# Writing the bulk loads of a row-maximum kernel with 32 KB source pieces over 16 KB destination rows

## The chip, the cores and the metric

One core of one Trainium2 chip. The time is microseconds of device time for one execution of the program; the span of the profile is about 1.8 us shorter, because it begins and ends with the instructions. All runs told here are of granted clock 1.0 on the one core.

## The reference

```python
def setup_inputs():
    batch, seq, dim = 32, 512, 1024
    return {"x": np.random.randn(batch, seq, dim).astype(np.float32)}

def reference(x):
    return np.max(x, axis=-1).astype(np.float32)
```

So 16384 rows of 4 KB (67.1 MB) are read once, and one number comes out of each row.

## The kernel before

Four consecutive rows (16 KB, contiguous in memory) go to each of the 128 partitions, which makes a tile of 2 MB. There are 32 tiles: 28 bulk ones, loaded and reduced whole, and four at the end, loaded in halves of 1 MB. Up to eight bulk loads are in flight.

```python
G = 4
xr = xf.rearrange("(t p g) d -> t p g d", p=P, g=G)
bulk = ctx.enter_context(tc.tile_pool(name="bulk", bufs=10))
...
for t in range(T):                       # T = 32
    if t < T - 4:
        xc = bulk.tile([P, G, D], F32)
        nc.sync.dma_start(out=xc, in_=xr[t])
        nc.vector.reduce_max(out=res[:, :, t], in_=xc, axis=X)
    else:
        for h in range(0, G, 2):
            xt = tailp.tile([P, 2, D], F32)
            nc.sync.dma_start(out=xt, in_=xr[t, :, h:h + 2, :])
            nc.vector.reduce_max(out=res[:, h:h + 2, t], in_=xt, axis=X)
# cut: four small transposes of the maxima and four stores
```

Of the kernel before, what the change touches and what calls it, by code (L numbers as in the profile page):

```python
# [1 line left out]

# [4 lines left out]


F32 = mybir.dt.float32
G = 4  # L10


@with_exitstack
def kernel(
    ctx: ExitStack,
    tc: tile.TileContext,
    x: bass.AP,
    out: bass.AP,
):
    nc = tc.nc  # L20
    P = 128
    X = mybir.AxisListType.X

    xf = x.flatten_outer_dims()
    N, D = xf.shape
    T = N // (P * G)


    xr = xf.rearrange("(t p g) d -> t p g d", p=P, g=G)
    of = out.flatten_outer_dims()  # L30

    bulk = ctx.enter_context(tc.tile_pool(name="bulk", bufs=10))
    tailp = ctx.enter_context(tc.tile_pool(name="tailp", bufs=5))
    once = ctx.enter_context(tc.tile_pool(name="once", bufs=1))


    res = once.tile([P, G, T], F32)
    turned = once.tile([P, 32, G], F32)

    for t in range(T):  # L40
        if t < T - 4:
            xc = bulk.tile([P, G, D], F32)
            nc.sync.dma_start(out=xc, in_=xr[t])  # L43
            nc.vector.reduce_max(out=res[:, :, t], in_=xc, axis=X)  # L44
        else:
            for h in range(0, G, 2):
# [4 lines that stand above are left out]
    for g in range(G):  # L51
        nc.vector.transpose(out=turned[:, :, g], in_=res[:, g, :])  # L52

    for q in range(P // 32):
        dst = bass.AP(
            tensor=of.tensor,
            offset=of.offset + q * 32 * G,
            ap=[[P * G, T], [1, 32 * G]],
        )
        eng = (nc.scalar, nc.sync)[q % 2]  # L60
        eng.dma_start(out=dst, in_=turned[q * 32:(q + 1) * 32, :, :].rearrange("p a g -> p (a g)"))


# [1 line left out]
_INS = ['x']  # L65
_OUTS = [((32, 512), 'float32')]


# [23 lines left out]
```

## Time and profile before

| | before |
|---|---|
| time, median of 4 runs | 168.15 us (167.98 to 168.31) |
| span of the profile | 166.3 us |
| VectorE busy | 142.0 us |
| a bulk reduction | 4.421 us |
| from one bulk reduction to the next | 4.894 us |
| last bulk reduction starts | 140.72 us |

The period of 4.894 us is worked out from the trace: the first bulk reduction starts at 8.580 us, the 28th at 140.719, and (140.719 - 8.580) / 27 = 4.894. All periods below are taken in this way.

From the page of the kernel before: the busy tenths of the DMA engines in 40 slices, the bytes moved, the packets, the queues, and the largest group of VectorE (busy us, mean ns | idle us just before, and who ended it):

```profile
DMA  5999999999999999999999999999999999999930
GB/s 177 402 433 437 441 437 429 410 426 441 433 429 414 426 441 433 426 414 429 441 433 422 422 426 441 433 422 422 426 441 433 422 418 418 422 424 420 422 154 16
DMA packets 5376, 67.18 MB, mean 404 GB/s; under 512 B 640, under 2 KB 768, under 8 KB 768
...
q1 hardware_dynamic: 5280, 67.14, 95.5%
...
L44 DVE TENSOR_REDUCE res<-xc 128x4 f32<-128x4096 f32 x28 | 123.8, 4421 | 21.3 <-DMA xc<-in_x_dram 21.3
```

The DMA engines are busy 90% or more of every slice between the first and the last two, and VectorE waits for them before every bulk reduction. The chain of waits that ended last (start us, us, what) says the same:

```profile
2.12 21.09 DMA xc<-in_x_dram
...
23.27 39.10 DMA xc<-in_x_dram
...
62.44 39.08 DMA xc<-in_x_dram
...
101.58 39.11 DMA xc<-in_x_dram
...
140.72 4.42 DVE res L44
145.14 15.36 DVE res L49 x7
```

One piece of the chain is one load from its issue to its landing, with eight loads in flight: eight tiles land in each 39.1 us. After the last bulk tile VectorE works without a pause to the end. Time taken off the period of a bulk load should therefore come off the total, 28 times, as long as VectorE still has to wait for it.

### The profile page before, as it was taken

Reading aid. Unit: us, or ns where it says so; the run is one execution under the profiler, and the core shown is the slowest. Engines: PE = TensorE matmul, PEld = TensorE weight load, DVE = VectorE, ACT = ScalarE, POOL = GpSimd, SP = SyncE. Lnnn points to the kernel's source line nnn. Section 1 sums busy time; section 2 is a strip of 40 time slices with the busy share of each in tenths; the row PEclk is TensorE's granted clock in tenths of the full one; section 3 lists DMA queues with packets and bytes.
Section 4 is the critical chain, followed back from the end, with each engine's and each line's share of the span. In section 5 each row is a group of like instructions: output and inputs, shape, how many; then the busy total and the mean of one; then the engine's idle time right before and its main releaser. Section 6 shows DMA issues by size and latency. Waiting matters only on the chain.

```text
span 166.3 us, 147 instructions
## 1 busy us (share of the span) xinstructions
DVE 142.0 (85%) x40; POOL 0.2 (0%) x4
## 2 busy tenths in 40 slices
DVE  0098888898888889888889988888988888999992
POOL 0000000000000000000000000000000000000000
DMA  5999999999999999999999999999999999999930
GB/s 177 402 433 437 441 437 429 410 426 441 433 429 414 426 441 433 426 414 429 441 433 422 422 426 441 433 422 422 426 441 433 422 418 418 422 424 420 422 154 16
DMA packets 5376, 67.18 MB, mean 404 GB/s; under 512 B 640, under 2 KB 768, under 8 KB 768
## 3 DMA queue, kind: packets, MB, share of 16 engines
q1 hardware_dynamic: 5280, 67.14, 95.5%
q10 hardware_dynamic: 96, 0.03, 0.1%
HBM read 67.11 MB, written 0.07 MB: 404 GB/s over the span
## 4 chain that ended last, share of the span: by engine, by line
DMA 83%; DVE 14%; SPq 1%; issue 0%; DVEq 0%
DMA xc<-in_x_dram 83%; DVE res L49 11%; DVE res L44 3%; SPq L43 1%; DVE turned L52 0%; DVEq L87 0%
## 5 line engine op out<-in xcount | busy, mean ns | idle before, releaser
L44 DVE TENSOR_REDUCE res<-xc 128x4 f32<-128x4096 f32 x28 | 123.8, 4421 | 21.3 <-DMA xc<-in_x_dram 21.3
L49 DVE TENSOR_REDUCE res<-xt 128x2 f32<-128x2048 f32 x8 | 17.7, 2274 | 0.0
L52 DVE STREAM_TRANSPOSE turned<-res 128x32 f32<-128x32 f32 x4 | 0.7, 213 | 0.1
L76 POOL MEMSET const-bfloat16-1.0<- 128x1 bf16 x1 | 0.1, 101 | 0.0
L76 POOL MEMSET const-uint8-127<- 128x1 uint8 x1 | 0.1, 101 | 0.0
L76 POOL MEMSET const-float32-0.0<- 128x1 f32 x1 | 0.1, 98 | 0.2 <-issue 0.2
L76 POOL MEMSET const-float32-1.0<- 128x1 f32 x1 | 0.1, 98 | 0.0
## 6 DMA issues: line engine op xcount, KB each, us to landing
xc<-in_x_dram SPq DMA_DIRECT2D x28, 2048.0 KB, 39.1
xt<-in_x_dram SPq DMA_DIRECT2D x8, 1024.0 KB, 28.3
out_dram<-turned SPq DMA_DIRECT2D x2, 16.0 KB, 1.5
out_dram<-turned ACTq DMA_DIRECT2D x2, 16.0 KB, 1.6
```

Of the source, the lines that this page charges most:

```text
L43: nc.sync.dma_start(out=xc, in_=xr[t])
L44: nc.vector.reduce_max(out=res[:, :, t], in_=xc, axis=X)
L49: nc.vector.reduce_max(out=res[:, h:h + 2, t], in_=xt, axis=X)
L52: nc.vector.transpose(out=turned[:, :, g], in_=res[:, g, :])
L76: nc = _bacc.Bacc("TRN2", target_bir_lowering=False, num_devices=1)
```

## The change

Let each bulk load read memory in 64 pieces of 32 KB, each of which covers the rows of two neighbouring partitions, while every partition still receives 16 KB. The DMA engines would then handle half as many source pieces (the prediction calls them read descriptors).

```diff
-    xr = xf.rearrange("(t p g) d -> t p g d", p=P, g=G)
-    of = out.flatten_outer_dims()
+    def stretch(first, rows):
+        piece = 8192
+        return bass.AP(
+            tensor=xf.tensor,
+            offset=xf.offset + first * D,
+            ap=[[piece, rows * P * D // piece], [1, piece]],
+        )
 ...
         if t < T - 4:
             xc = bulk.tile([P, G, D], F32)
-            nc.sync.dma_start(out=xc, in_=xr[t])
+            nc.sync.dma_start(out=xc.rearrange("p g d -> p (g d)"), in_=stretch(t * P * G, G))
             nc.vector.reduce_max(out=res[:, :, t], in_=xc, axis=X)
```

(`xr` stays, for the tail, and so does `of`; both only move. Blank lines are left out.)

More of the change, by code (lines that the diff above doesn't have):

```diff
@@ L38 @@
     turned = once.tile([P, 32, G], F32)
+    xr = xf.rearrange("(t p g) d -> t p g d", p=P, g=G)
     for t in range(T):
```

## The prediction

> **What bounds the kernel.** The loads. The chain of waits that ended last is 83% "DMA xc<-in_x_dram" and 14% VectorE; VectorE is busy 142.0 of 166.3 us, and each of its 28 bulk reductions takes 4421 ns after some 0.48 us of waiting for a load (21.3 us in all, 8.6 of it before the first). The chain walks in steps of 39.10 us for 8 tiles: one 2 MB tile lands every 4.888 us, 429 GB/s. Only after the last bulk tile lands (140.7 us) is VectorE the limit: 4.4 us for that tile, eight tail reductions back to back (2.27 us each), transposes and the store.
>
> **What the change touches.** Only the read side of the 28 bulk loads: 64 source pieces of 32 KB instead of 128 of 16 KB. Bytes, destinations, issue order, waits, buffers and VectorE work stay (the order of instructions is identical). The Trainium skill, "DMA: Bandwidth & Descriptors", section "Why a DMA increments its semaphore by 16 and not by 1", says the engine count is the largest up to 16 that divides both sides' slowest dimension: 64 and 128 still give 16. I expect each engine to keep the same bytes and the same eight partitions, with 4 reads per tile instead of 8.
>
> **What there is to gain.** The trace's DMA records: a 16 KB packet takes 611 to 619 ns, an 8 KB packet 309 to 313, a 4-byte completion write 9. Extrapolating (estimate: 2 x 309 - 611) gives some 7 ns fixed per descriptor. A second estimate: the same page's "Where 436 GB/s comes from" puts the ceiling at 435.2 GB/s, or 4.819 us per tile; the trace shows 4.888, so 69 ns per tile are overhead: 8 x 7.5 ns plus the 9 ns completion.
>
> If the fixed cost belongs to the read descriptor, halving the reads saves 4 x 7.5 = 30 ns per tile, 28 x 30 = 0.84 us. If it belongs to the write descriptor, or the hardware cuts the pair at the smaller piece, nothing is saved. The floor (no overhead at all) would be 28 x 69 ns = 1.9 us, so over 2% faster (3.4 us) is nearly excluded.
>
> **On the critical path.** All of any saving: the last bulk tile lands earlier by the sum, and the VectorE tail, which follows without idle time, starts that much earlier. VectorE (4.42 us) stays under the load period (4.86). The start (first reduction at 8.6 us) should be unchanged or a tenth or two worse, because the first reads (0.8 to 1.8 us in the trace) become larger.
>
> **Prediction.** 167.5 us (range 166.6 to 168.5), from 168.14. Faster by over 2%: 0.02; within 2%: 0.94; slower by over 2%: 0.04.
>
> **What would show it.** 1792 bulk records of 32 KB near 1215 ns (or still 3584 of 16 KB if records count writes); landings every 4.86 us instead of 4.888 (38.9 for 8 tiles); VectorE idle before bulk reductions down to about 20.5 us; last bulk reduction starting near 139.9 instead of 140.7; the tail of 22.3 us unchanged.
>
> **What would make it wrong.** [...] If a 32 KB read against two 16 KB writes stalls the engine, packets would exceed 2 x 614 ns and the kernel be a per cent or so slower. If the period is unchanged, the fixed cost sits on the write side.

## The result, and the profile after

168.19 us (168.14 to 168.27, 4 runs) against 168.15 us: ratio 1.0003, 95% interval 0.9985 to 1.002. Here and below, a ratio is the mean time of one kernel's runs over the mean of the other's from the same rounds, so it is not quite the ratio of the medians quoted beside it.

The same lines of the page of the kernel after, with the same columns:

```profile
DMA  5999999999999999999999999999999999999930
...
DMA packets 5376, 67.18 MB, mean 404 GB/s; under 512 B 640, under 2 KB 768, under 8 KB 768
...
q1 hardware_dynamic: 5280, 67.14, 95.5%
...
L53 DVE TENSOR_REDUCE res<-xc 128x4 f32<-128x4096 f32 x28 | 123.8, 4422 | 21.4 <-DMA xc<-in_x_dram 21.4
```

And its chain of waits:

```profile
23.35 39.11 DMA xc<-in_x_dram
...
62.52 39.10 DMA xc<-in_x_dram
...
101.68 39.10 DMA xc<-in_x_dram
...
140.81 4.42 DVE res L53
145.23 15.36 DVE res L58 x7
```

Nothing moved: the same number of packets to the last one, the same steps of 39.1 us, the same idle time. A count that does not change by a single packet, after an edit that was to halve 3584 reads, asks for a look at what was built. The records of the transfers show 3584 packets of 16 KB in both traces. The built program explains it. The access patterns of the first bulk load, written as [step, count] in elements, slowest first, are:

```
before   source [[4096, 128], [1, 4096]]   destination [[4096, 128], [1, 4096]]
after    source [[4096, 128], [1, 4096]]   destination [[4096, 128], [1, 4096]]
```

All 28 bulk loads are like this. A comparison of the two built programs, instruction by instruction, found no difference except the places in the source (line numbers and call stacks). The load call brings both sides of a transfer to one form before it makes the instruction; the 64 stretches of 32 KB lie end to end in memory, so they were cut again to match the 128 destination rows. **The edit never reached the chip, so this run says nothing about 32 KB reads.** The ratio of 1.0003 is that of a program to itself, and so a measure of the noise.

That leaves the question that the edit was meant to ask. I had three theories for it. R: the fixed cost of a piece belongs to the read side, so that real 32 KB reads would save time. W: it belongs to the write side. N: no fixed cost per piece sets the period.

### The profile page after: what moved, and what is told of

Read it like the earlier page. It is cut to its first block, busy times and chain, and to the rows that moved or that the text cites. A ratio compares the mean times of both kernels' runs of the same rounds, so it can differ in the third digit from the quotient of the medians.

```text
span 166.4 us, 147 instructions
## 1 busy us (share of the span) xinstructions
DVE 142.0 (85%) x40; POOL 0.2 (0%) x4
## 2 busy tenths in 40 slices
DMA packets 5376, 67.18 MB, mean 404 GB/s; under 512 B 640, under 2 KB 768, under 8 KB 768
## 3 DMA queue, kind: packets, MB, share of 16 engines
q1 hardware_dynamic: 5280, 67.14, 95.5%
## 4 chain that ended last, share of the span: by engine, by line
DMA 83%; DVE 14%; SPq 1%; issue 0%; DVEq 0%
DMA xc<-in_x_dram 83%; DVE res L58 11%; DVE res L53 3%; SPq L52 1%; DVE turned L61 0%; DVEq L96 0%
## 6 DMA issues: line engine op xcount, KB each, us to landing
xc<-in_x_dram SPq DMA_DIRECT2D x28, 2048.0 KB, 39.1
```

## The experiments

The pattern can be put into the instruction after the front end has made it. The following block stands in the launch code, just before the program is handed over, and gives the 28 bulk loads a source and a destination pattern of choice. It also turns off the flag `ant_dge_precooked`, because the front end had set it for its own pattern. Below, each experiment gives only SRC and DST.

```diff
+    import copy
+    for block in (bl for f in nc.m.functions for bl in f.blocks):
+        for k, ins in enumerate(block.instructions):
+            if type(ins).__name__ == "InstDMACopy" and [list(d) for d in ins.ins[0].ap] == [[4096, 128], [1, 4096]]:
+                block.instructions[k] = copy.replace(
+                    ins,
+                    ins=[copy.replace(ins.ins[0], ap=SRC)],
+                    outs=[copy.replace(ins.outs[0], ap=DST)],
+                    ant_dge_precooked=False,
+                )
     r = _run(nc, [arrays], core_ids=[0])
```

What could not be tried: reads smaller than the writes. Reads of 8 KB or 1 KB against 16 KB rows do not compile ("DMA instruction must read and write same number of elements (or, for a plain HW-DGE copy, read elements that are whole multiples of the write element)"). Reads of 64 KB failed at the same place. So the read side can only be made equal to the write side or wider.

### Real 32 KB reads, and their control

read32_write16 (from the kernel after):

```diff
-SRC = [[4096, 128], [1, 4096]]
+SRC = [[8192, 64], [1, 8192]]
 DST = [[4096, 128], [1, 4096]]
```

> In the built program the changed kernel is identical to the one before: the front end turned the 64 pieces of 32 KB back into 128 reads of 16 KB. This run writes the pattern [64 pieces x 8192 elements] into the 28 bulk instructions after the build, so that the reads really are 32 KB (flag ant_dge_precooked off). Theory R (fixed cost on the read side): 8 to 4 reads per engine and tile, landings every 4.858 us instead of 4.888, about 0.84 us less than read16_write16_plain (0.995). Theory W (fixed cost per write, or per piece both sides are cut to) and theory N (no fixed cost sets the period): equal within 0.1%, landings every 4.888 us. If the engines' share of the destinations does not follow the wider reads, the result is wrong[...].

read16_write16_plain (from the kernel before; only the flag is changed):

```diff
 SRC = [[4096, 128], [1, 4096]]
 DST = [[4096, 128], [1, 4096]]
-ant_dge_precooked=True
+ant_dge_precooked=False
```

> Control: the kernel before with the same rewriting of the 28 bulk instructions but unchanged patterns, only the flag ant_dge_precooked off. All theories: 168.15 us within 0.3 us, landings every 4.888 us; the issue of one bulk load on the queue of SP may take longer than 0.33 us, which eight loads in flight hide except at the start.

Measured on one chip, both results right: 168.42 us with 32 KB reads, 168.47 us for the control, 168.12 us for the kernel before. Against before the ratios are 1.0015 (1.0002 to 1.0027) and 1.0016 (1.0003 to 1.0029). From the page of read32_write16:

```profile
DMA packets 3585, 67.18 MB, mean 403 GB/s; under 512 B 641, under 2 KB 769, under 8 KB 769
...
q1 hardware_dynamic: 3488, 67.14, 95.1%
...
L53 DVE TENSOR_REDUCE res<-xc 128x4 f32<-128x4096 f32 x28 | 123.8, 4422 | 21.6 <-DMA xc<-in_x_dram 21.6
```

and two steps of its chain of waits:

```profile
23.59 39.09 DMA xc<-in_x_dram
...
62.75 39.09 DMA xc<-in_x_dram
```

Now the reads are 32 KB: queue q1 has 3488 packets instead of 5280, exactly 1792 fewer, and the transfer records show 1792 of 32 KB with a median of 1.227 us in the steady part, twice the 0.611 to 0.619 us of a 16 KB record. So the packets of a trace count reads. The steps are still 39.09 us, and the period is 4.894 us (control 4.896). The same lines of the control read16_write16_plain:

```profile
L44 DVE TENSOR_REDUCE res<-xc 128x4 f32<-128x4096 f32 x28 | 123.8, 4422 | 21.7 <-DMA xc<-in_x_dram 21.7
```

```profile
23.62 39.10 DMA xc<-in_x_dram
...
62.79 39.10 DMA xc<-in_x_dram
```

Theory R asked for 30 ns less per tile and 0.84 us in all; 2 ns and 0.05 us were found, and 0.05 us is less than the spread of either kernel's five runs. R falls.

The right result and the unchanged period also agree with the prediction's reading of the Trainium skill, "DMA: Bandwidth & Descriptors", section "Why a DMA increments its semaphore by 16 and not by 1": 64 source pieces and 128 partitions still spread over all 16 engines (the packets of q1 fill 95.1% of the time of 16 engines, against 95.5% in the kernel before).

The control explains the 0.3 us by which both lose: issuing one bulk load takes 472 ns on the queue of SP instead of 328, and the long wait of the chain starts at 2.60 us instead of 2.12. That is the flag, not the reads.

### Smaller writes, with and without smaller reads

read16_write1 (from the kernel before):

```diff
-SRC = [[4096, 128], [1, 4096]]
-DST = [[4096, 128], [1, 4096]]
+SRC = [[4096, 128], [1, 1], [1, 4096]]
+DST = [[4096, 128], [256, 16], [1, 256]]
```

> Reads stay 16 KB, each is written in 16 pieces of 1 KB (same destination bytes). Theory W: 120 more write pieces per engine and tile at about 7.5 ns, an estimate from the first trace: +0.9 us per tile, landings every 5.8 us, about 193 us in all. Theory R: landings every 4.888 us, 168.2 us. Theory N: the same 168.2 us.

read1_write1 (from the kernel before):

```diff
-SRC = [[4096, 128], [1, 4096]]
-DST = [[4096, 128], [1, 4096]]
+SRC = [[4096, 128], [256, 16], [1, 256]]
+DST = [[4096, 128], [256, 16], [1, 256]]
```

> Both sides in 1 KB pieces. Theory W (cost per write only, or per pair of pieces): the same as read16_write1, about 193 us. Theory R (reads alone cost): about 193 us while read16_write1 stays at 168.2. If both sides cost on their own: slower than read16_write1. Theory N: 168.2 us.

Measured: 199.83 us (ratio 1.1885) and 199.97 us (ratio 1.1894), both right. The pages, first read16_write1:

```profile
DMA packets 5376, 67.18 MB, mean 339 GB/s; under 512 B 640, under 2 KB 768, under 8 KB 768
...
L44 DVE TENSOR_REDUCE res<-xc 128x4 f32<-128x4096 f32 x28 | 123.8, 4422 | 53.0 <-DMA xc<-in_x_dram 53.0
```

then read1_write1:

```profile
DMA packets 59136, 67.18 MB, mean 339 GB/s; under 512 B 640, under 2 KB 58112, under 8 KB 58112
...
L44 DVE TENSOR_REDUCE res<-xc 128x4 f32<-128x4096 f32 x28 | 123.8, 4422 | 53.4 <-DMA xc<-in_x_dram 53.4
```

Three landings from the timeline of read16_write1 (start us, us; the interval is the period):

```profile
64.01 4.42 DVE L44 TENSOR_REDUCE res<-xc 128x4 f32<-128x4096 f32 x1 [1.59 <-DMA xc<-in_x_dram]
70.04 4.42 DVE L44 TENSOR_REDUCE res<-xc 128x4 f32<-128x4096 f32 x1 [1.61 <-DMA xc<-in_x_dram]
76.06 4.42 DVE L44 TENSOR_REDUCE res<-xc 128x4 f32<-128x4096 f32 x1 [1.59 <-DMA xc<-in_x_dram]
```

The second kernel has 11 times as many packets as the first and is no slower beyond 0.14 us in 200. The first has not one packet more than the kernel before and is 32 us slower. The number that the page prints is the number of reads, and here it is not the one that matters. The periods are 6.022 and 6.023 us against 4.896 of the control. With 128 writes per engine and tile instead of 8, that is (6.022 - 4.896) us / 120 = 9.4 ns per write. Theories R and N fall; W stays, with 9.4 ns in place of the 7.5 that I had estimated (the reason why both runs came out at 200 and not at 193 us).

One thing this does not show: that a short read is free. In every kernel here the reads are as long as the writes or longer. A cost of reads that runs beside the writes and is no larger than theirs would stay hidden, and no run excludes it.

### Is it a fixed time per write?

read16_write4 (from the kernel before):

```diff
-SRC = [[4096, 128], [1, 4096]]
-DST = [[4096, 128], [1, 4096]]
+SRC = [[4096, 128], [1, 1], [1, 4096]]
+DST = [[4096, 128], [1024, 4], [1, 1024]]
```

> Is the cost of a write piece one fixed time? From the two 1 KB runs: (6.022 - 4.896) us / 120 extra write pieces per engine and tile = 9.4 ns each. Reads of 16 KB written in 4 pieces of 4 KB are 24 extra pieces: +0.225 us, bulk reductions every 5.121 us, 28 x 0.225 = 6.3 us more than read16_write16_plain, about 174.8 us. If small pieces cost more each than large ones, less: at 2 ns a piece 169.8 us.

Measured: 174.61 us (ratio 1.039), right. The period is 5.120 us, so (5.120 - 4.896) us / 24 = 9.3 ns per extra write of 4 KB: the same price as for 1 KB. (This run was made on another chip than its control; the kernel before took 168.07 us on this chip and 168.12 us on the control's.) A cost of the longer pattern as such, whatever the number of writes, is excluded by the two results: 1.126 us for 120 extra writes and 0.224 us for 24 lie on a straight line through zero, within 2 ns. From its page:

```profile
L44 DVE TENSOR_REDUCE res<-xc 128x4 f32<-128x4096 f32 x28 | 123.8, 4421 | 27.8 <-DMA xc<-in_x_dram 27.8
```

The transfer records of the engines say the same: the median record of a 16 KB read takes 614 ns with one write (control), 644 ns with four and 756 ns with sixteen, which is 10 and 9.5 ns per extra write.

This run also answers an objection to W, that the queue which makes the descriptors is the slow part. The start of its chain of waits:

```profile
0.73 0.63 SPq L43
...
1.42 0.58 SPq L43
...
2.05 0.59 SPq L43
...
2.68 0.66 SPq L43
...
3.39 1.80 SPq L43
...
5.24 4.87 SPq L43
```

The first four loads, together 4 x 512 = 2048 writes, were issued in 2.6 us; only then was the queue held up. The fifth issue took 1.80 us, and the next ones nearly a whole period each. So 2048 writes, as many as one load of the 1 KB kernels has, are issued in less than half of the 6.02 us which such a load takes. As far as the times of issue tell, the queue waits for the engines, not the engines for the queue. A slow queue working beside the transfers would also show only when it became slower than they are, while this cost is there from 24 extra writes on.

### Larger writes

With four rows per partition no write can be longer than 16 KB. A load of 4 MB with eight rows per partition allows 32 KB. Both kernels below read 32 KB and differ only in the writes. They put the maxima of the two halves where those of two tiles belonged. Their outputs are wrong, which doesn't matter for the times.

Both (from the kernel before):

```diff
+    xw = xf.rearrange("(t p g) d -> t p g d", p=P, g=2 * G)
-    bulk = ctx.enter_context(tc.tile_pool(name="bulk", bufs=10))
+    bulk = ctx.enter_context(tc.tile_pool(name="bulk", bufs=5))
 ...
         if t < T - 4:
-            xc = bulk.tile([P, G, D], F32)
-            nc.sync.dma_start(out=xc, in_=xr[t])
-            nc.vector.reduce_max(out=res[:, :, t], in_=xc, axis=X)
+            if t % 2:
+                continue
+            xc = bulk.tile([P, 2 * G, D], F32)
+            nc.sync.dma_start(out=xc, in_=xw[t // 2])
+            nc.vector.reduce_max(out=res[:, :, t], in_=xc[:, :G, :], axis=X)
+            nc.vector.reduce_max(out=res[:, :, t + 1], in_=xc[:, G:, :], axis=X)
```

tile4m_write16 has besides (the block above, for the 14 loads of 4 MB):

```diff
+SRC = [[8192, 128], [1, 1], [1, 8192]]
+DST = [[8192, 128], [4096, 2], [1, 4096]]
```

> Control of tile4m_write32; the rows of each pair of tiles land in another order, so the result is wrong on purpose. One load of 4 MB for two tiles, cut into 16 KB writes (reads of 32 KB): a pair of tiles should land every 2 x 4.896 = 9.78 to 9.79 us. Total about 172.5 us: the last bulk load leaves two reductions of 4.42 us to do instead of one.

tile4m_write32 has instead:

```diff
+SRC = [[8192, 128], [1, 8192]]
+DST = [[8192, 128], [1, 8192]]
```

> The same with writes of 32 KB, which one partition row of the 4 MB tile holds; result wrong on purpose as in its control. If the fixed cost is 9.4 ns per write piece and still holds there: 8 pieces fewer per engine and load, 75 ns less of 9.78 us, over 14 loads 1.05 us less than tile4m_write16 (ratio 0.994). If the cost were not a fixed time per piece but only of small pieces: equal within 0.1%. Under the read theory, which the earlier runs speak against: equal, as both read 32 KB.

Measured: 172.35 us and 171.21 us (ratios to the kernel before 1.0253 and 1.0186). A step of the chain of waits is four loads of 4 MB here; tile4m_write16:

```profile
51.72 40.15 DMA xc<-in_x_dram
...
140.84 4.42 DVE res L47
```

and tile4m_write32:

```profile
51.22 39.76 DMA xc<-in_x_dram
...
139.59 4.42 DVE res L47
```

The periods are 9.789 and 9.714 us. The difference of 75 ns over 8 writes is again 9.4 ns, and the total fell by 1.14 us where 1.05 was expected. Not all of the fall is the period: 0.28 us of it is there when the first load lands (13.31 against 13.59 us), of which 8 writes at 9.4 ns explain 0.08; the rest was not followed up. Neither kernel is fast as a whole: the last bulk load leaves two reductions of 4.42 us to VectorE instead of one, as foreseen.

The price is thus one number over the whole range tried: 9.4, 9.3 and 9.4 ns per write and engine, measured with writes of 1, 4 and 32 KB against 16 KB. An estimate from it: a bulk tile without it and without the 9 ns completion write seen in the records would take 4.896 - 8 x 0.0094 - 0.009 = 4.812 us, that is 436 GB/s. This agrees with the 435.2 GB/s that the Trainium skill, "DMA: Bandwidth & Descriptors", section "Where 436 GB/s comes from", gives as the ceiling.

### A version that uses it

head_write32: the first 14 tiles as 7 loads of 4 MB, from the plain load call and without the block above; then loads of 2 MB as before, so that VectorE can catch up; the tail unchanged. Its core:

```diff
+    H = 7
+    xw = xf.rearrange("(t p g) d -> t p g d", p=P, g=2 * G)
+    for t2 in range(H):
+        xc = bulk.tile([P, 2 * G, D], F32)          # bulk: 5 buffers of 4 MB
+        nc.sync.dma_start(out=xc, in_=xw[t2])
+        nc.vector.reduce_max(out=head[:, :, t2], in_=xc, axis=X)
-    for t in range(T):
+    for t in range(2 * H, T):
+        # cut: bulk loads of 2 MB, each into one half of a 4 MB buffer; tail as before
+        if t == T - 8:
+            # cut: 8 transposes of head and 4 small stores on the queue of ACT
```

> A version with a right result that uses what the runs showed: the first 14 tiles are loaded as 7 loads of 4 MB with 32 KB per partition on both sides, the rest as before; their maxima are turned and stored in mid-kernel, so that the tail is as before. Write theory: a 4 MB load takes 9.715 us (tile4m_write32) instead of 2 x 4.896, so 7 x 0.076 = 0.53 us less than before: about 167.6 us, ratio 0.997. If the longer reductions of the head are not caught up by VectorE before the tail (it gains 0.47 us on each later tile), or if the stores in mid-kernel disturb the loads, no gain. Not over 2% in any case.

Measured: 167.31 us (167.20 to 167.38) against 168.14 us, right result, ratio 0.9951 (0.9938 to 0.9965). From its timeline:

```profile
13.28 8.69 DVE L49 TENSOR_REDUCE head<-xc 128x8 f32<-128x8192 f32 x1 [12.02 <-DMA xc<-in_x_dram]
22.90 8.69 DVE L49 TENSOR_REDUCE head<-xc 128x8 f32<-128x8192 f32 x1 [0.93 <-DMA xc<-in_x_dram]
...
140.00 4.42 DVE L58 TENSOR_REDUCE res<-xc 128x4 f32<-128x4096 f32 x1 [0.48 <-DMA xc<-in_x_dram]
```

The last bulk reduction starts at 140.00 us instead of 140.72, and VectorE waits 0.48 us before it, so it had caught up. By the seventh load the head is 0.72 us ahead (71.46 us, where the 14th tile of the kernel before landed at 72.18); 0.16 us of that is there at the first landing (13.28 against 13.44). The expected 0.53 us counted only the period; why the first load lands earlier was not followed up. Of the 0.83 us by which the median fell, 0.11 us is more than the loads account for; its place was not traced. The gain is real but small: half a per cent.

## Why the prediction was right or wrong

- **The time: right, by luck.** 168.19 us lies in the range of 166.6 to 168.5, and no change of 2% was forecast or came. But the range held "no change" (168.14), and the run was the old program once more, so the hit confirms nothing about reads. The central 167.5 us held a gain of 0.6 us that did not come.
- **What bounds the kernel: right.** The loads set the period, and a saving in them reaches the end: in head_write32 the last bulk reduction starts 0.72 us earlier, and the total is 0.83 us lower. The period itself was put at 4.888 us and is 4.894 or 4.896: I divided a step of the chain by eight without the 0.07 us of issue between two steps.
- **What the change touches: the step that failed.** The prediction says "64 source pieces of 32 KB instead of 128 of 16 KB". In the built program there are 128 of 16 KB in both. I had compared the order of the instructions but not the operands of the loads, and "the order of instructions is identical" was truer than I knew.
- **The sign named in advance worked, and its reading would not have.** "1792 bulk records of 32 KB ... (or still 3584 of 16 KB if records count writes)": 3584 appeared, and the reason was a third one, that the reads had not changed. read32_write16 shows that records count reads. Likewise "if the period is unchanged, the fixed cost sits on the write side" turned out true as far as it could be tested, but the unchanged period of the kernel after was no evidence for it.
- **Read side or write side: left open by the prediction, settled by the runs for reads no shorter than the writes.** With real 32 KB reads the gain is 0.05 us instead of 0.84. Reads 16 times as many cost nothing that could be measured; 16 times as many writes cost 32 us.
- **The fixed cost: mis-sized.** Estimated at 7 to 7.5 ns, measured at 9.3 to 9.4 ns. The period of 4.888 us was 8 ns too short (6 with 4.894), which is about 1 ns per write. The other estimate, 2 x 309 - 611, cannot bear the weight: with the median records of the same trace, 313 and 614 ns, it gives 12.
- Still open: whether the price belongs to a write descriptor or to any piece to which both sides are cut, and whether reads have a cost of their own that stays hidden beside the writes. These cases differ only when reads are smaller than writes, which does not compile.

## What to carry to other kernels

When an edit concerns how a transfer is cut, read the access patterns of the built instruction, or count the packets of that queue, before you explain a time; a call that brings both sides to one form can undo the edit without a word. For loads that keep all DMA engines busy, count the writes per engine, not the packets that the page prints: here each write cost 9.4 ns, so runs in SBUF should be as long as the layout allows, and reads that are no shorter than the writes may be cut as is convenient (16 KB against 1 KB under writes of 1 KB, and 32 KB against 16 KB under writes of 16 KB, made no difference). At 16 KB per write that price is 8 x 9.4 ns in 4896, or 1.5% of the period, and nobody should hope for more from it.

## What the Trainium skill lacked or had wrong

- "DMA: Bandwidth & Descriptors", section "Why small descriptors are slow (HBM only)", gives a fixed cost of about 3 cycles per packet and does not say which side pays; nor do the nearest measured figures of the skill, about 10.5 ns per packet in small loads issued from GpSimd (same page, section "Measured (HBM→SBUF, 128 partitions, SWDGE, issued from GpSimd)") and 42 to 43 ns for a descriptor of 1 KiB (page "Advanced Engine Details and Errata", under "Clock Domains"). The runs show 9.3 to 9.4 ns per write and engine, for writes of 1 to 32 KB, and nothing measurable per read as long as the reads are no shorter than the writes (59136 packets instead of 5376 for 0.14 us). A piece of 1 KB took 47 ns in all (6.022 us / 128).
- "DMA: Bandwidth & Descriptors", section "Why a DMA increments its semaphore by 16 and not by 1", mentions in passing a load whose reads are widened over several rows. The end of that page says that the shape of the tile decides the descriptors when the program is built, which comes near; but no page that I read says that the load call cuts the two sides alike (64 pieces of 32 KB became 128 of 16 KB), nor that such a load runs with the right result and the same period once the pattern is in the instruction (4.894 us against 4.896).
- No page that I read says that the transfer records of a trace count reads: 3585 packets with 32 KB reads, 5376 with 16 KB reads even when each was written in 16 pieces.
